# High and low part of x in one 512-column product, where one stream of tokens stands alone

## The chip, the cores and the metric

The kernel runs on one core of one Trainium2 chip. The metric is the device time of one execution in microseconds (us); the kernel before took 2060.02 us (median of 3 runs, 2059.41 to 2060.64). The engines are named as the profile names them: PE is TensorE (its weight loads are PEld), DVE is VectorE, ACT is ScalarE, POOL is GpSimd, SP issues most DMAs.

## The reference

The program is two transformer blocks of two layers each, on 256 tokens of width 1024, in float32. Both blocks are mostly gated feed-forward layers:

```
rmsnorm(h, g) = h * rsqrt(mean(h*h) + eps) * g
swiglu(x, w1, w3, w2) = (silu(x @ w1) * (x @ w3)) @ w2        # 1024 -> 2 x 2816 -> 1024
first block, per layer:  h = h + 0.5 * swiglu(rmsnorm(h, g0), ...)
                         h = h + mixer(rmsnorm(h, g1))         # attention of two kinds
                         h = h + 0.5 * swiglu(rmsnorm(h, g2), ...)
second block, per layer: x = layer_norm(ALPHA*x + gate1 * mixing(modulate(x)))
                         x = layer_norm(ALPHA*x + gate2 * swiglu_2(modulate(x), ...))
                         # the same for a context stream of 256 tokens, in the first layer alone
```

The second block's shifts, scales and gates ("modulation") come from a product of a vector with `w_mod`, 1024 x 6144 per layer.

## The kernel before

**Products.** Activations lie feature-major: 128 features on the partitions, 256 tokens (S) in the columns. A weight block is 128 x 128. Float32 is reached with three products of a faster type (FR): weight and activation are each split into a high part and the rest (low part), and `mm3` (L317 to L326) issues high x high, high x low, low x high, which add into one PSUM bank (L324, L325, L326). Each is a matmul with its own weight load. In most layers x has 256 columns; where both streams of the second block share a layer's weights, 512.

**Weights.** `Weights` streams one array in chunks of 8 blocks (128 x 1024, 512 KB), in the order in which they are used. Three staging tiles `wst` are filled by DMA; `prepare` makes the high part `whi` on ACT (L279) and the low part `wlo` on DVE (L280). Four chunks of split weights are kept (NHL = 4): the fifth chunk is split when PE has done with one of the four. There are 540 chunks.

**Feed-forward layers.** Up: for each of 22 hidden blocks j, `slab_fm` runs 8 k-blocks for both halves (c = 0, 1) into one bank, with the weights stored so that k=0 of c=0, k=0 of c=1, k=1 of c=0 and so on follow each other. In the first block (`ffn1_layer`, four layers, h0, h2, h3 and h5) DVE then multiplies the bank with the norm's factor `r` (L863), ACT takes the silu (L865), DVE the product (L866), and `split` makes high and low of the result (L330 on ACT, L331 on DVE). In the second block (`up_gen`) ACT and DVE read the bank directly (L1508, L1509). Down: for each of 8 output blocks m, 22 (or 11) k-blocks go into the first half of a bank, and DVE adds it to the residual (L797, L1543); in layers that follow at once, ACT and DVE then make high and low of the next input (`HI`, `LO`: L513, L514).

**Beside the layers.** `self.bg` holds background work that `step()` pushes on after each j and m: in the first three layers the product with `w_mod` (DVE L724, ACT L727, POOL L728), in the fourth (h5) the norm of the context stream (`ctx_init`: a sum on DVE, L1443 and L1445, one matmul with ones, L1447, then eight blocks of L1452 and further work).

**Order.** The build hands all instructions to a scheduler that simulates the engines with costs of its own and writes each engine's queue in the order in which its simulation starts them. On the chip each queue runs strictly in that order. PSUM has 4 banks under the name mm, 3 under sc (also used as st and tp) and one, half.

## Time and profile before

| | |
|---|---|
| runs shown | 2059.41, 2060.02, 2060.64 us |
| profiled execution | 2062.72 us, of which the span of instructions is 2060.9 us |
| PE busy | 1989.5 us (97%), 15355 matmuls in the profile |
| weight loads busy | 1851.9 us (90%) |
| DVE busy | 1524.9 us (74%) |
| ACT busy | 1134.6 us (55%) |
| DMA | 172 GB/s on average |
| granted clock of TensorE, mean | 0.988 |

An engine's busy time is the union of its instructions. Matmuls overlap in the profile (each row shows its whole passage), so PE can look busy without running at its best: what a product costs is read from the distance of the starts of two that follow each other. A row of the timeline gives start and duration in us, then engine, line, operation, out<-in by the program's names and the shape, partitions x elements.

### The profile page before, as it was taken

To read this page: it belongs to the slowest core of one execution; us is meant where nothing else is said; L and a number is where in the kernel's file an instruction comes from. 1 tells how busy PE (TensorE), PEld (TensorE's weight loads), DVE (VectorE), ACT (ScalarE), POOL (GpSimd) and SP (SyncE) were. 2 spreads that over 40 slices of the span, in tenths; PEclk is the share of its full clock that TensorE was granted. 3 is DMA by queue.
4 is the path that set the end of the run, shared out by engine and by line. 5 is a ranking of instruction groups with operands and counts; after the bars stand their busy time and mean duration, and the time that the engine had idled before them with its cause. 6 is when DMAs were issued, how large, how long until landed. Compare 5 with 4: busy or idle time off the path is not lost. (4 is left out here: it accounts for less than half of the span.)

```text
span 2060.9 us, 39210 instructions
## 1 busy us (share of the span) xinstructions
PE 1989.5 (97%) x15355; PEld 1851.9 (90%) x15355; DVE 1524.9 (74%) x2680; ACT 1134.6 (55%) x2028; POOL 408.4 (20%) x305
## 2 busy tenths in 40 slices
PE   8998999999999999999999999999999999989997
PEld 8988999989999998999999777988888889869997
DVE  6797797998599768886686978666665679776554
ACT  5464587555466548555556866533443455855443
POOL 1223041321033111210330112302230013112002
PEclk9999999999999999999999999999999999999999
DMA  6785645876577563556642323475555653125553
GB/s 219 260 266 171 202 144 184 281 249 215 185 232 229 187 216 110 184 172 188 188 145 73 104 80 118 144 250 169 160 163 164 216 169 103 50 83 156 183 183 103
DMA packets 117114, 355.39 MB, mean 172 GB/s; under 512 B 21782, under 2 KB 27625, under 8 KB 116481
## 3 DMA queue, kind: packets, MB, share of 16 engines
q1 hardware_dynamic: 115472, 344.54, 51.9%
q10 hardware_dynamic: 1456, 8.36, 1.1%
q8 instruction: 120, 1.97, 0.4%
q14 instruction: 66, 0.53, 0.1%
HBM read 351.66 MB, written 8.90 MB: 175 GB/s over the span
## 5 line engine op out<-in xcount | busy, mean ns | idle before, releaser
L280 DVE TENSOR_TENSOR wlo<-wst,whi 128x1024 fp32r<-128x1024 f32 x540 | 709.2, 1314 | 329.4 <-ACT whi L279 327.1
L324 PE MATMUL mm<-HI,whi 128*128 128x256 f32 (+1 forms) x2944 | 865.2, 296 | 12.7 <-ACT whi L279 8.4
L326 PE MATMUL mm<-HI,wlo 128*128 128x256 f32 (+1 forms) x2944 | 863.9, 294 | 6.0 <-DVE wlo L280 6.0
L325 PE MATMUL mm<-LO,whi 128*128 128x256 f32 (+1 forms) x2944 | 865.4, 295 | 1.0 <-DVE LO L1413 0.9
L279 ACT ACTIVATE whi<-wst 128x1024 fp32r<-128x1024 f32 x540 | 570.2, 1056 | 524.8 <-PE mm L325 292.7
L324 PEld LDWEIGHTS mm<-HI,whi 128*128 128x128 f32 x2944 | 564.2, 193 | 38.3 <-issue 11.4
L326 PEld LDWEIGHTS mm<-HI,wlo 128*128 128x128 f32 x2944 | 566.1, 192 | 21.8 <-DVE wlo L280 7.3
L325 PEld LDWEIGHTS mm<-LO,whi 128*128 128x128 f32 x2944 | 566.6, 193 | 18.7 <-issue 6.9
L326 PE MATMUL mm<-ghi,wlo 128*128 128x256 f32 (+1 forms) x1000 | 289.1, 289 | 4.7 <-DVE wlo L280 4.7
L324 PE MATMUL mm<-ghi,whi 128*128 128x256 f32 (+1 forms) x1000 | 287.7, 289 | 1.3 <-ACT ghi L330 1.3
L325 PE MATMUL mm<-glo,whi 128*128 128x256 f32 (+1 forms) x1000 | 288.6, 289 | 0.2 <-DVE glo L331 0.2
L728 POOL TENSOR_TENSOR macc<-macc,mp 128x1024 f32<-128x1024 f32 (+1 forms) x70 | 167.9, 2398 | 447.2 <-ACT mp L727 298.1
L326 PEld LDWEIGHTS mm<-ghi,wlo 128*128 128x128 f32 x1000 | 192.8, 193 | 8.4 <-DVE wlo L280 5.1
L324 PEld LDWEIGHTS mm<-ghi,whi 128*128 128x128 f32 x1000 | 192.4, 193 | 4.3 <-issue 1.5
L325 PEld LDWEIGHTS mm<-glo,whi 128*128 128x128 f32 x1000 | 192.7, 193 | 2.8 <-issue 1.1
L724 DVE SCALAR_TENSOR_TENSOR macc<-mw,sc,macc 128x512 f32<-128x512 f32 (+1 forms) x126 | 168.3, 1336 | 25.6 <-DMA mw<-in_wmod 20.4
L325 PE MATMUL mm<-wlo,HI 128*128 128x256 f32 x352 | 100.6, 286 | 4.0 <-DVE wlo L280 4.0
L324 PE MATMUL mm<-whi,HI 128*128 128x256 f32 x352 | 101.1, 288 | 0.0
L326 PE MATMUL mm<-whi,LO 128*128 128x256 f32 x352 | 100.2, 286 | 0.0
L727 ACT ACTIVATE mp<-mw,sc 128x1024 f32<-128x1024 f32 (+1 forms) x70 | 67.4, 973 | 27.5 <-DMA mw<-in_wmod 18.5
L527 POOL TENSOR_TENSOR sacc<-sacc,w 128x256 f32<-128x256 f32 x36 | 33.6, 932 | 236.7 <-ACT w L523 235.5
L330 ACT ACTIVATE ghi<-w 128x256 fp32r<-128x256 f32 (+1 forms) x120 | 51.1, 426 | 49.8 <-DVE w L866 47.1
(425 smaller groups left out, 2502.5 us busy)
## 6 DMA issues: line engine op xcount, KB each, us to landing
wst<-in_wall SPq DMA_DIRECT2D x540, 512.0 KB
mw<-in_wmod SPq DMA_DIRECT2D x48, 512.0 KB
mw<-in_wmod SPq DMA_DIRECT2D x96, 256.0 KB
brep<-bvec ACTq DMA_DIRECT2D x16, 384.0 KB
nab<-rrep SPq DMA_DIRECT2D x24, 96.0 KB
bias<-brep SPq DMA_DIRECT2D x4, 512.0 KB
bias<-brep SPq DMA_DIRECT2D x8, 256.0 KB
rrep<-in_rpb ACTq DMA_DIRECT2D x4, 348.8 KB
```

The costliest lines, as they stand in the source:

```text
L279: self.marks.append(self.nc.scalar.activation(hi, src, AF.Copy))
L280: self.nc.vector.tensor_tensor(lo, src, hi.bitcast(FT), op=OP.subtract)
L324: nc.tensor.matmul(ps, wh, xh, start=first, stop=False, skip_group_check=True)
L325: nc.tensor.matmul(ps, wh, xl, start=False, stop=False, skip_group_check=True)
L326: self.last = nc.tensor.matmul(ps, wl, xh, start=False, stop=last, skip_group_check=True)
L330: self.marks = [self.nc.scalar.activation(hi, src, AF.Copy), self.nc.vector.tensor_tensor(lo, src, hi.bitcast(FT), op=OP.subtract)]
L527: nc.gpsimd.tensor_tensor(st["acc"], st["acc"], sq, op=OP.add)
L724: nc.vector.scalar_tensor_tensor(acc[:, i], w, s, acc[:, i], op0=OP.mult, op1=OP.add)
L727: nc.scalar.activation(t, w, AF.Copy, scale=s)
L728: nc.gpsimd.tensor_tensor(acc[:, i], acc[:, i], t, op=OP.add)
```

## The change

- Where only one stream is multiplied, x is stored with high and low side by side (256 + 256 columns), and `mm3` issues two products a block in place of three: low weight x high x into the first half of a bank, then high weight x both (512 columns) into the whole bank. The bank then holds the sum in two halves, which have to be added.
- It applies in: the down projections of all four layers of the first block; the up projection of the fourth (h5), which has no product with `w_mod` beside it; the one-stream up projections of the second block (12 hidden blocks in its first layer, 22 in its second); and its one-stream down projections.
- Down: DVE adds both halves to the residual, one instruction each. Up: `joined` copies one half out on ACT and adds the other on DVE. Each half (c = 0, 1) is a bank of its own, and the weights are stored with the 8 k-blocks of c=0 first, so that a bank belongs to one chunk. In h5 and in the second block's second layer every third such bank is taken from sc.
- In h5 (`normed_up`) the first four hidden blocks multiply with `r` after the join; meanwhile, after j=1 and j=2, a normalised copy of the input is made (`xn`: one DVE instruction, one on ACT and one on DVE for each of 8 m), and from j=4 on the products read that, so the multiplication with `r` falls away.

```diff
+def _ffn1s(w1, w3, j0, j1):
+    out = []
+    for j in range(j0, j1):
+        for w in (w1, w3):
+            out.append(w[:, j * 128:(j + 1) * 128].reshape(KB, 128, 128).transpose(1, 0, 2))
+    return out
...
-        hi = self.split.tile([128, 1024], FR, name="whi")
-        lo = self.split.tile([128, 1024], FR, name="wlo")
-        self.marks.append(self.nc.scalar.activation(hi, src, AF.Copy))
-        self.nc.vector.tensor_tensor(lo, src, hi.bitcast(FT), op=OP.subtract)
-        self.hl[i] = (hi, lo)
+        w = self.split.tile([128, 2, 1024], FR, name="whl")
+        self.marks.append(self.nc.scalar.activation(w[:, 0], src, AF.Copy))
+        self.nc.vector.tensor_tensor(w[:, 1], src, w[:, 0].bitcast(FT), op=OP.subtract)
+        self.hl[i] = w
...
     def mm3(self, ps, w, x, first, last, swap=False):
-        (wh, wl), (xh, xl) = w, x
         nc = self.nc
         if swap:
-            (wh, wl), (xh, xl) = (xh, xl), (wh, wl)
+            w, x = x, w
+        wh, wl = w[:2]
+        xh, xl = x[:2]
+        if len(ps.shape) == 2 and len(xh.shape) == 2 and ps.shape[1] == 2 * xh.shape[1]:
+            nc.tensor.matmul(ps[:, :S], wl, xh, start=first, stop=False, skip_group_check=True)
+            self.last = nc.tensor.matmul(ps.rearrange("p (h t) -> p h t", h=2), wh, x[2], start=False, stop=last,
+                                         skip_group_check=True)
+            return
         nc.tensor.matmul(ps, wh, xh, start=first, stop=False, skip_group_check=True)
         nc.tensor.matmul(ps, wh, xl, start=False, stop=False, skip_group_check=True)
         self.last = nc.tensor.matmul(ps, wl, xh, start=False, stop=last, skip_group_check=True)
...
+    def wide(self, x, n, spare=False):
+        ps = self.ps("sc" if spare and self.turn % 3 == 2 else "mm")
+        self.turn += 1
+        for k in range(n):
+            self.mm3(ps, self.W.block(self.wpos + k), self.at(x, k), k == 0, k == n - 1)
+        self.wpos += n
+        return ps
+    def joined(self, dst, ps):
+        c = self.w1()
+        self.nc.scalar.activation(c, ps[:, S:], AF.Copy)
+        self.nc.vector.tensor_tensor(dst, ps[:, :S], c, op=OP.add)
...
-                nc.vector.scalar_tensor_tensor(hm, ps, scale, hm, op0=OP.mult, op1=OP.add)
+                for c in (0, S):
+                    nc.vector.scalar_tensor_tensor(hm, ps[:, c:c + S], scale, hm, op0=OP.mult, op1=OP.add)
...
+    def normed_up(self, st, pool, g, gain):
+        nc = self.nc
+        x = st["hl"]
+        y = pool.tile([128, KB, 2, S], FR, name="xn")
+        y = y[:, :, 0], y[:, :, 1], y
+        turns = {1: range(4), 2: range(4, KB)}
+        for j in range(FB):
+            t = self.w2()
+            sl = self.w1()
+            for c in range(2):
+                ps = self.wide(x if j <= NORM else y, KB, True)
+                if j == 0 and c == 0:
+                    self.rms_stat(st, D)
+                self.joined(t[:, c], ps)
+                if j <= NORM:
+                    nc.vector.tensor_tensor(t[:, c], t[:, c], st["r"], op=OP.mult)
+                if c == 0:
+                    nc.scalar.activation(sl, t[:, 0], AF.Silu)
+            nc.vector.tensor_tensor(sl, sl, t[:, 1], op=OP.mult)
+            self.split(g[:, j, 0], g[:, j, 1], sl)
+            self.step()
+            for m in turns.get(j, ()):
+                w = self.w1()
+                nc.vector.scalar_tensor_tensor(w, self.h[:, m], gain[:, m:m + 1], st["r"], op0=OP.mult, op1=OP.mult)
+                self.split(y[0][:, m], y[1][:, m], w)
...
+            if idx == 3:
+                self.normed_up(st, mp, g, self.vec[:, _VEC["norm_g"] + 40:_VEC["norm_g"] + 48])
-            for j in range(FB):
+            for j in range(FB if idx < 3 else 0):
...
-                ps = self.ps("mm")[:, :S]
-                for k in range(FB):
-                    self.mm3(ps, self.W.block(self.wpos + k), (gh[:, k], gl[:, k]), k == 0, k == FB - 1)
-                evict(m, ps)
-                self.wpos += FB
+                evict(m, self.wide(parts2(g), FB))
...
-                ps, = self.slab_fm([self.hl(1 - i)])
+                t = self.w2()
+                for c in range(2):
+                    self.joined(t[:, c], self.wide(self.hl(1 - i), KB, len(js) == FB))
                 sl = self.w1()
-                a, b = ps[:, 0], ps[:, 1]
+                a, b = t[:, 0], t[:, 1]
...
+                if len(streams) == 1:
+                    self.mm3(ps, w, parts(g(k, streams[0])), k == 0, k == nk - 1)
                     continue
...
-                evict(i, m, ps[:, c:c + S])
+                evict(i, m, ps[:, (1 - i) * S:(2 - i) * S] if len(streams) == 2 else ps)
```

How the queues are written, in h5's up projection. On PE at its start, before (mm_10213 is j=0, mm_10290 is j=1; the `whi` and `wlo` numbers name chunks):

```order
L324 MATMUL mm_10213<-HI_82,whi_10065 128x256
L325 MATMUL mm_10213<-LO_83,whi_10065 128x256
L326 MATMUL mm_10213<-HI_82,wlo_10066 128x256
...
L324 MATMUL mm_10290<-HI_82,whi_10148 128x256
L325 MATMUL mm_10290<-LO_83,whi_10148 128x256
...
L324 MATMUL mm_10213<-HI_82,whi_10095 128x256
```

and after (mm_9454 and mm_9487 are the two halves of j=0, sc_9521 and mm_9548 those of j=1):

```order
L351 MATMUL mm_9454<-HL_82,whl_9307 128x256
L352 MATMUL mm_9454<-HL_82,whl_9307 128x512
L351 MATMUL mm_9487<-HL_82,whl_9336 128x256
...
L351 MATMUL mm_9548<-HL_82,whl_9455 128x256
...
L585 MATMUL st_9476<-sacc_9350,ones_94 128x256
...
L351 MATMUL sc_9521<-HL_82,whl_9388 128x256
```

Before, two hidden blocks advance together over the first four k; after, three halves advance together over all k (the bank sc_9521 comes behind the matmul of the norm's statistics).

On PE around the matmul of the context's sum, before (mm_10443 is j=3, mm_10516 j=4):

```order
L326 MATMUL mm_10443<-HI_82,wlo_10371 128x256
L1447 MATMUL st_10362<-sacc_10358,ones_95 128x256
L324 MATMUL mm_10443<-HI_82,whi_10370 128x256
L325 MATMUL mm_10443<-LO_83,whi_10370 128x256
...
L324 MATMUL mm_10516<-HI_82,whi_10400 128x256
```

and after (mm_9713 is the second half of j=3, sc_9633 the second of j=2, sc_9749 and mm_9775 are j=4, mm_9810 and sc_9836 j=5):

```order
L352 MATMUL mm_9713<-HL_82,whl_9607 128x512
L1524 MATMUL st_9581<-sacc_9577,ones_94 128x256
L351 MATMUL sc_9633<-HL_82,whl_9522 128x256
...
L351 MATMUL sc_9749<-xn_9451,whl_9634 128x256
L351 MATMUL mm_9775<-xn_9451,whl_9687 128x256
...
L351 MATMUL mm_9810<-xn_9451,whl_9714 128x256
...
L351 MATMUL sc_9836<-xn_9451,whl_9750 128x256
```

The matmul of the context's sum (L1447, now L1524) stood inside j=3; now it stands behind both halves of j=3 and ahead of the second half of j=2, and behind it come four halves that read `xn`, woven k by k.

On DVE in the same place, before (L1443 and L1445 make the context's sum):

```order
L280 TENSOR_TENSOR wlo_10401<-wst_10295,whi_10400 128x1024
L331 TENSOR_TENSOR glo_10212<-w1_10353,ghi_10211 128x256
L1443 TENSOR_TENSOR sacc_10358<-cx_10287 128x256
L863 TENSOR_TENSOR w2_10430<-mm_10369,rstd_10277 128x512
L1445 TENSOR_TENSOR sacc_10358<-sacc_10358,cx_10287 128x256
```

and after (L297 is the split of weights, L915 with the L382 behind it makes `xn`, L372 is the join):

```order
L297 TENSOR_TENSOR whl_9714<-wst_9610,whl_9714 128x1024
L382 TENSOR_TENSOR ghl_9450<-w1_9520,ghl_9450 128x256
L1520 TENSOR_TENSOR sacc_9577<-cx_9516 128x256
L1522 TENSOR_TENSOR sacc_9577<-sacc_9577,cx_9516 128x256 x2
L1529 TENSOR_TENSOR ex_9517<-cx_9516,w1_9583 128x256
L915 SCALAR_TENSOR_TENSOR w1_9588<-h_83,vec_84,rstd_9479 128x256
...
L372 TENSOR_TENSOR w2_9604<-mm_9606,w1_9628 128x256
L907 TENSOR_TENSOR w2_9604<-w2_9604,rstd_9479 128x256
L297 TENSOR_TENSOR whl_9750<-wst_9637,whl_9750 128x1024
```

The context's sum now stands behind the weights of chunk whl_9714 (j=5), and `xn` behind the sum.

## Rows read from the trace of the kernel before

**Rows 1.** The page's head and its first part: busy time of each engine.

```profile
span 2060.9 us, 39210 instructions
PE 1989.5 (97%) x15355; PEld 1851.9 (90%) x15355; DVE 1524.9 (74%) x2680; ACT 1134.6 (55%) x2028; POOL 408.4 (20%) x305
```

**Rows 2.** Windows: stretch, length, then busy us (x instructions) by engine, clock, DMA.

```profile
core 0: us, PE busy (x) PEld busy (x) DVE busy (x) ACT busy (x) POOL busy (x), PEclk, DMA share, GB/s
491.90:555.30 63.40, 63.40 (x530) 63.40 (x529) 36.99 (x40) 29.21 (x38) 5.57 (x6) 1.00 0.65 216
830.00:960.70 130.70, 130.70 (x1079) 129.95 (x1078) 105.24 (x152) 73.98 (x123) 21.83 (x20) 1.00 0.57 182
...
1300.00:1320.00 20.00, 20.00 (x164) 19.20 (x163) 16.19 (x35) 12.32 (x26) 4.37 (x4) 1.00 0.47 151
1920.00:1983.00 63.00, 63.00 (x527) 63.00 (x527) 34.30 (x44) 29.32 (x45) 0.00 (x0) 1.00 0.57 184
```

**Rows 3.** Timeline of PE, the last down projection, 256 columns.

```profile
2043.79 0.28 PE L325 MATMUL mm<-glo,whi 128*128 128x256 f32 x1
...
2046.07 0.28 PE L326 MATMUL mm<-ghi,wlo 128*128 128x256 f32 x1
```

**Rows 4.** Timeline of PE, 512 columns: alone, and behind 256-column products.

```profile
1414.69 0.40 PE L324 MATMUL mm<-ghi,whi 128*128 128x512 f32 x1
...
1418.14 0.28 PE L324 MATMUL mm<-early_qcT,whi 128*128 128x256 f32 x1
...
1483.64 0.39 PE L326 MATMUL mm<-HI,wlo 128*128 128x512 f32 x1
...
1486.81 0.39 PE L325 MATMUL mm<-LO,whi 128*128 128x512 f32 x1
```

**Rows 5.** Lines by shape: xcount | busy us, mean ns (L280, L863, L331, L279: 831 to 961).

```profile
L280 DVE TENSOR_TENSOR wlo<-wst,whi 128x1024 fp32r<-128x1024 f32 x45 | 55.6, 1235 | 21.4 <-ACT whi L279 21.2
L863 DVE TENSOR_TENSOR w<-mm,rstd 128x512 f32<-128x512 f32 x22 | 15.1, 688 | 2.9 <-PE mm L326 2.9
L331 DVE TENSOR_TENSOR glo<-w,ghi 128x256 fp32r<-128x256 f32 x21 | 8.8, 418 | 0.0
...
L1509 DVE TENSOR_TENSOR w<-w,mm 128x256 f32<-128x256 f32 x34 | 14.0, 413 | 0.0
L797 DVE SCALAR_TENSOR_TENSOR h<-mm,h 128x256 f32<-128x256 f32 x24 | 10.1, 421 | 11.7 <-PE mm L326 11.7
L1543 DVE SCALAR_TENSOR_TENSOR ex<-mm,modv,ex 128x256 f32<-128x256 f32 x24 | 11.5, 480 | 22.6 <-PE mm L326 22.6
...
L1508 ACT ACTIVATE w<-mm 128x256 f32<-128x256 f32 x34 | 12.4, 366 | 0.0
L279 ACT ACTIVATE whi<-wst 128x1024 fp32r<-128x1024 f32 x45 | 47.6, 1057 | 42.9 <-PE mm L325 24.8 <-issue 15.0 <-PE st L534 1.6
```

**Rows 6.** Timeline of DVE and PE, start of h5's up projection.

```profile
832.76 3.12 DVE L514 SCALAR_TENSOR_TENSOR LO<-h,vec,HI 128x256 fp32r<-128x256 f32 x4
835.80 1.76 DVE L280 TENSOR_TENSOR wlo<-wst,whi 128x1024 fp32r<-128x1024 f32 x1
...
851.43 0.42 DVE L1445 TENSOR_TENSOR sacc<-sacc,cx 128x256 f32<-128x256 f32 x1
...
854.51 0.60 PE L1447 MATMUL st<-sacc,ones 128*128 128x256 f32 x2
```

**Rows 7.** Windows, h5's up projection where DVE is fullest.

```profile
907.90:931.30 23.40, 23.40 (x198) 23.40 (x197) 23.40 (x39) 16.34 (x26) 0.00 (x0) 1.00 0.61 188
```

**Rows 8.** Windows, start of the down projection of h0.

```profile
150.00:175.00 25.00, 19.00 (x152) 18.18 (x151) 24.96 (x17) 14.38 (x18) 17.56 (x6) 0.99 0.49 164
175.00:180.00 5.00, 4.92 (x23) 4.92 (x24) 4.53 (x7) 1.40 (x3) 0.00 (x0) 0.50 0.57 176
```

**Rows 9.** Timeline of DVE, the last residual.

```profile
2046.39 0.48 DVE L1543 SCALAR_TENSOR_TENSOR ex<-mm,modv,ex 128x256 f32<-128x256 f32 x1 [7.37 <-PE mm L326]
```

More of the change, by code (lines that the diff above doesn't have):

```diff
@@ L289, in block, with parts @@
             self.prepare()
-        hi, lo = self.hl[h]
         c = (i % 8) * 128
-        return hi[:, c:c + w * 128], lo[:, c:c + w * 128]
+        return parts(self.hl[h][:, :, c:c + w * 128])
+def parts(both):
+    return both[:, 0], both[:, 1], both
 class Body:
@@ L298, in __init__ @@
         self.last = None
+        self.turn = 0
         self.rests = [None, None]
```

134 lines of the change are left out of this document (70 added, 64 removed).

## The prediction

> **What bounds the kernel now.** The page's first part comes first: PE is busy 97% of the span, DVE 74%, ACT 55% [rows 1]. PE's share alone proves little, since its matmuls overlap, so the next view is the windows by stage: in the down projection of h2, in h5's up projection and in the last layer's up projection PE is busy for the whole stretch, while DVE has 20 to 46% of its time free [rows 2]. Then the timeline, for the distance of starts. In the last down projection 20 products of 256 columns start between 2043.79 and 2046.07, so 2.28/19 = 0.120 us each [rows 3], and the stretch of h2 (63.4 us, 528 products) gives the same 0.120. PE there goes from one product to the next with no hole: these stages last as long as their products. For 512 columns, where both streams share a layer, 15 starts lie between 1483.64 and 1486.81, 3.17/14 = 0.226 us each; where stretches of 256-column products alternate with them it is 15 in 3.45 us, 0.230 [rows 4]. Doubling the columns costs 0.106 to 0.110 us, so some 13 ns of the 0.120 belong to a product whatever its width. That part is what the change is about.
>
> **The change part by part.** *Products.* The blocks concerned: 8 x 22 in each of the four down projections of the first block (704), 22 x 16 in h5's up projection (352), 12 x 16 and 22 x 16 in the one-stream up projections of the second block (544), 2 x 8 x 11 and 8 x 22 in its one-stream down projections (352): 1952. A block costs 3 x 0.120 = 0.360 us now and 0.120 + 0.226 = 0.346 after, so it gains 13.6 ns and all of them 26.5 us. Bounds: with 0.230 for the wide product 10 ns or 19.5 us, with 0.118 for the narrow one (0.344) 15.6 ns or 30.5 us. I take 26.5, since 0.120 and 0.226 each come from unbroken stretches of their kind.
>
> The Trainium skill ("TensorE: Matmul & The Clock Gate", section "Back-to-back issue gap") puts the warm distance at columns / 2.4 GHz plus 2.5 ns; by it a block would go from 327.5 to 325 ns, the gain would be 4.9 us, and with the losses worked out below the sum 2067.0 us, slower than before. The rows differ from it, with 120 and 226 ns where it has 109 and 216, and they decide.
>
> *Where the gain does not count.* From 150 to 175 us the down projection of h0 is paced by DVE, busy for all of 25 us while PE gets through 152 instructions, about 50 blocks [rows 8]; their 13.6 ns are lost, 0.7 us.
>
> *Residuals.* Each m gets one more DVE instruction, 0.42 us (first block) or 0.48 (second) [rows 5]. It lies beside the next m's products (22 x 0.346 = 7.6 us) and costs nothing, except behind the very last m, where nothing is left to do but the final norm: +0.48 us [rows 9].
>
> *Joins.* Each hidden block gets two copies on ACT (0.37) and two additions on DVE (0.41); in h5 the first four get two multiplications of 0.42 in place of one of 512 columns [rows 5]. The cover is PE's 5.55 us a hidden block. In the last layer DVE is busy 34.3 of 63 us and ACT 29.3 [rows 2]; with 0.8 us more a block both stay under 75%. In the second block's first layer DVE is busy 16.2 of 20 us [rows 2] and comes to some 95%; the weights are split up to three chunks (8 us) ahead, which hides such a stretch. I take 0 (up to 3 us if that cover is gone).
>
> *The start of h5's up projection.* Here I expect a loss: the work for `xn` (16 instructions on DVE, 8 on ACT) arrives within three hidden blocks, and the written order makes PE wait for it. Before, PE waits nowhere in this stage [rows 2]. Step by step, from the order and the durations of [rows 5, 6]:
> - PE starts at 831.0 and now weaves two halves; input blocks beyond the sixth come late (DVE makes four of them until 835.9), and the third half begins with a product that reads the low weights of the fourth chunk, split on DVE until 835.80 + 1.76 = 837.5. Until then PE has 12 blocks, 4.2 us of 6.5: about 2.4 us idle. (Before, it had all of k = 0 to 3 of two hidden blocks, 16 blocks of 0.36, for that time.)
> - The three woven halves hold three of four chunks to their end, and the next chunks queue on ACT and DVE (1.06 + 1.24 us each) with joins and the norm's factor between them: 1.5 us.
> - The matmul of the context's sum now stands ahead of a whole half of j=2. PE reaches it when j=3 is done. DVE, in its queue, first has to split chunk whl_9714, whose place comes free only then: ACT 1.06, DVE 1.24, the low part of j=1's result 0.42, the sum 3 x 0.42, and hand-overs: 4.2 us idle. Before, the sum's last step started at 851.43 and PE came to the matmul at 854.51 [rows 6], no wait.
> - Behind it PE has 8 blocks that don't read `xn` and 16 that need it up to m=3 (8.3 us), then it wants m=4. From the sum to `xn` of m=4 DVE has 18 instructions of 0.42 and a split of 1.24, 8.8 us, with about 2 us of waits for ACT's parts: 2 us idle.
> - The four halves woven there end together and give their four chunks back together: the next split (1.06 + 1.24) has only three blocks (1.0 us) as cover: 1.3 us.
>
> Sum 11.4 us. Bounds: 0, if everything behind PE's waits turns out early enough, and 20, if the waits also bring the clock down: in h0 PE had a hole between 165 and 175, and the stretch after it ran at a granted clock of 0.50, 23 instructions in 5 us [rows 8].
>
> *Sum.* 26.5 - 0.7 - 0.48 - 11.4 = 13.9 us off. The profiled execution, on which all this rests, took 2062.72 us, 1.8 more than its span and 2.7 more than the median of the runs; the differences carry over: 2060.0 - 13.9 = 2046.2 us.
>
> **The rivals.**
> - *The cover holds in h5.* The scheduler wrote this order because its own simulation saw little waiting; if the real queues fit as well, only 1.2 us come off the gain: 2034.7 us. For it: DVE is on average only 105 of 131 us busy in that stage, and four hidden blocks at 100% DVE cost PE nothing before [rows 2, 7]. Against: the waits above are waits for something ordered behind something, which average load does not cure. Chance 0.24.
> - *More of it.* The same pattern (woven halves, slots that come free together) also stands at the starts of the second block's up projections; if each of the two costs another 4.5 us, 2055. Against: there DVE has no `xn` to make. Chance 0.10.
> - *Columns alone count.* If a product's cost went with its columns, a block would stay at 0.360 and only the losses would remain: 2060.0 + 0.5 + 11.4 = 2071.9 us, slower. The rows speak against it, 0.226 is not 0.240 [rows 4]. Chance 0.03.
> - *DVE becomes the bound of h5's up projection* (the slower side I hold likeliest). DVE's 105 us there [rows 2] grow by 44 joins (18.2), 8 multiplications (3.3) and 16 instructions for `xn` (6.7) and lose 22 of 0.69 (15.1 [rows 5]): 118 us, while PE's stage shrinks to 126. It decides from 126 on, 7% more than these durations; each percent beyond costs 1.2 us. To lose the other stages' gain and 4 us besides it would have to reach some 143 us, 21% more, as happens to single splits beside POOL (1.76 and not 1.24 at 835.80 [rows 6]); then 2065. POOL works 22 of the 131 us. Chance 0.05.
>
> **How the numbers follow.** My forecast gets 0.58, the rivals 0.24, 0.10, 0.03 and 0.05. 0.2% is 4.1 us, about what a measurement of this kernel can tell from no change. Faster means under 2055.9: all of the forecast, the first rival, and half of the second, 0.87; the same: the second's other half and a little of the last, 0.07; slower 0.06. The range runs from 2033, a little under the first rival, to 2056, a little over the second; the forecast's own is 2041 to 2052, with 9 to 15 us lost in h5 or the gain a few us off.
>
> **What the profile after would show.** PE's lines: 1952 products fewer, pairs whose starts are 0.120 and 0.226 apart, and the down projections of h2, h3 and h5 61.0 us long in place of 63.4. In h5's up projection: holes of PE ahead of the context's sum (4 us) and within j=4 and j=5, and a stage of about 137 us in place of 130.7 (126 if the cover holds). The forecast falls if the pair costs 0.36, if h5's stage is not longer than before, or if a stage that the change leaves alone moves by several us because the scheduler wrote its queues anew.

## The result and the profile after

| | before | after |
|---|---|---|
| runs, median (range) | 2060.3 us (2059.4 to 2062.8) | 2082.5 us (2080.7 to 2084.0) |
| profiled execution | 2062.7 us | 2082.8 us |
| granted clock, mean | 0.988 | 0.982 |

The change makes the kernel slower: the ratio of the times is 1.0109, with a 95% interval of 1.0095 to 1.0122. That is some 22 us more, where 14 us less were forecast.

The head of the page after, to be read against [rows 1]:

```profile
span 2081.0 us, 35637 instructions
PE 1988.5 (96%) x13403; PEld 1754.3 (84%) x13403; DVE 1580.8 (76%) x2850; ACT 1171.9 (56%) x2148; POOL 420.7 (20%) x305
```

Some 1950 products are gone (15355 - 13403), and PE is as long busy as before, while the span grew by 20 us. So about 20 us are new idle time of PE. That PE's busy time did not fall fits with products at half clock: mean clocks of 0.988 and 0.982 mean about 25 us more at 0.50, and a pair of products takes 0.64 us there in place of 0.35. The windows show where the time went (columns as in [rows 2]): the down projections of h2 and h3, h5's up projection, its two worst places, and the start of an up projection in the second block's first layer.

```profile
492.20:554.30 62.10, 62.10 (x354) 53.93 (x353) 40.14 (x47) 29.01 (x38) 6.10 (x6) 1.00 0.69 222
687.90:749.10 61.20, 61.20 (x355) 53.90 (x354) 41.05 (x54) 28.89 (x38) 6.13 (x6) 1.00 0.60 196
827.90:973.40 145.50, 134.03 (x716) 113.51 (x715) 111.61 (x197) 87.71 (x171) 19.85 (x20) 0.95 0.49 160
850.90:855.90 5.00, 0.11 (x2) 0.04 (x1) 3.66 (x7) 1.36 (x2) 0.00 (x0) 0.85 0.76 229
896.00:902.00 6.00, 5.91 (x19) 5.08 (x20) 2.88 (x7) 2.87 (x8) 1.61 (x3) 0.50 0.27 94
1328.70:1336.00 7.30, 3.02 (x11) 2.04 (x11) 7.15 (x18) 4.64 (x12) 2.59 (x3) 0.75 0.43 150
```

The down projections got shorter, h2's 62.1 for 63.4 us and h3's 61.2 for 63.5, which was before:

```profile
688.50:752.00 63.50, 63.50 (x532) 63.50 (x531) 38.38 (x47) 29.20 (x38) 5.57 (x6) 1.00 0.59 191
```

h5's up projection is 145.5 us long for 130.7, though DVE is busy for only 112 of them. Its waits on PE, from the view that sums waits by what ended them (engine, line, waited for: us in total, times, longest):

```profile
PE st L1524 <- DVE sacc L1522: 4.9, 1, 4.9
PE mm L351 <- DVE whl L297: 2.8, 3, 1.7
PE mm L351 <- DVE w L372: 2.8, 1, 2.8
PE sc L351 <- ACT xn L381: 0.4, 1, 0.4
```

These four are 10.9 us. The longest is the wait for the context's sum, which the prediction named; the third, 2.8 us for a join (L372), it did not name. Here it is in the timeline, on PE, then on ACT, then on DVE:

```profile
892.86 0.40 PE L352 MATMUL mm<-xn,whl 128*128 128x512 f32 x1
896.09 0.55 PE L351 MATMUL mm<-xn,whl 128*128 128x256 f32 x1 [2.83 <-DVE w L372]
896.44 0.63 PE L352 MATMUL mm<-xn,whl 128*128 128x512 f32 x1
896.87 0.42 PE L351 MATMUL mm<-xn,whl 128*128 128x256 f32 x1
897.08 0.63 PE L352 MATMUL mm<-xn,whl 128*128 128x512 f32 x1
```

```profile
893.30 1.06 ACT L296 ACTIVATE whl<-wst 128x1024 fp32r<-128x1024 f32 x1 [1.46 <-PE mm L352]
894.26 0.40 ACT L1268 ACTIVATE w<-ex 128x256 f32<-128x256 f32 x1
894.57 0.36 ACT L371 ACTIVATE w<-mm 128x256 f32<-128x256 f32 x1
```

```profile
894.39 1.23 DVE L297 TENSOR_TENSOR whl<-wst,whl 128x1024 fp32r<-128x1024 f32 x1 [0.92 <-ACT whl L296]
895.53 0.42 DVE L372 TENSOR_TENSOR w<-mm,w 128x256 f32<-128x256 f32 x1
```

The written order names what these are. On PE the halves stand as mm_9871, mm_9897, sc_9932, mm_9958, sc_10019, mm_9993 and, behind the wait, mm_10056, which needs the bank of mm_9871, since mm has four banks. On ACT (left) and DVE (right) it has:

```
L296 ACTIVATE whl_10057<-wst_9962 128x1024              L297 TENSOR_TENSOR whl_10057<-wst_9962,whl_10057 128x1024
L1268 ACTIVATE w1_9865<-ex_9517 128x256                 L372 TENSOR_TENSOR w2_9869<-mm_9871,w1_9893 128x256
L371 ACTIVATE w1_9893<-mm_9871 128x256
```

The join of mm_9871, which PE had finished five halves (14 us) earlier, stands behind the split of chunk whl_10057. That split waits until PE gives a chunk back at the end of mm_9993 (893.3). Then split on ACT, copy, split on DVE and addition run in a row, and only then PE has a bank. The loop costs PE 2.8 us here; behind it the granted clock is 0.50 for 6 us, and pairs start 0.64 us apart where they should have 0.35.

Each join cost what it was priced at [rows 5], in h5:

```profile
L372 DVE TENSOR_TENSOR w<-mm,w 128x256 f32<-128x256 f32 x29 | 12.1, 421 | 8.4 <-ACT w L371 8.3
```

Waits stand also in the second block's first layer, in a stretch (the last window above) whose mean clock is 0.75. Here is PE at the start of the second stream's hidden blocks, where the input (HL) and the weights' low parts come late:

```profile
1331.25 0.62 PE L351 MATMUL mm<-HL,whl 128*128 128x256 f32 x3 [0.96 <-ACT HL L1489]
1332.90 0.55 PE L351 MATMUL mm<-HL,whl 128*128 128x256 f32 x1 [1.03 <-DVE whl L297]
1334.93 0.80 PE L352 MATMUL mm<-HL,whl 128*128 128x512 f32 x1 [1.48 <-DVE HL L1490]
```

Next come products, PE in the down projections of h2 and of h3, and then the end of the kernel on DVE:

```profile
550.93 0.40 PE L352 MATMUL mm<-ghl,whl 128*128 128x512 f32 x1
551.16 0.28 PE L351 MATMUL mm<-ghl,whl 128*128 128x256 f32 x1
551.28 0.40 PE L352 MATMUL mm<-ghl,whl 128*128 128x512 f32 x1
...
552.70 0.40 PE L352 MATMUL mm<-ghl,whl 128*128 128x512 f32 x1
...
699.73 0.39 PE L352 MATMUL mm<-ghl,whl 128*128 128x512 f32 x1
...
703.89 0.39 PE L352 MATMUL mm<-ghl,whl 128*128 128x512 f32 x1
```

```profile
2065.82 1.00 DVE L1626 SCALAR_TENSOR_TENSOR ex<-mm,modv,ex 128x256 f32<-128x256 f32 x2 [6.78 <-PE mm L352]
```

Five pairs start between 550.93 and 552.70, so a pair costs 0.354 us in h2, not 0.346. In h3 it is twelve between 699.73 and 703.89, 0.347 us: the same alternation of shapes has two prices in one run. The last residual is two instructions in 1.00 us for one of 0.48 [rows 9].

### The profile page after: what moved, and what is told of

It reads as the page before. It is cut to its first block, busy times and chain, and to the rows that moved or that the text cites. A ratio compares the mean times of both kernels' runs of the same rounds, so it can differ in the third digit from the quotient of the medians.

```text
span 2081.0 us, 35637 instructions
## 1 busy us (share of the span) xinstructions
PE 1988.5 (96%) x13403; PEld 1754.3 (84%) x13403; DVE 1580.8 (76%) x2850; ACT 1171.9 (56%) x2148; POOL 420.7 (20%) x305
## 4 chain that ended last, share of the span: by engine, by line
PE 72%; DVE 13%; issue 5%; ACT 4%; DMA 3%; POOL 1%; SPq 0%; ACTq 0%; DVEq 0%; POOLq 0%
PE mm L352 17%; PE mm L355 12%; PE mm L357 11%; PE mm L356 11%; PE mm L351 9%; DVE whl L297 4%; DMA wst<-in_wall 3%; PE sc L352 2%; DVE macc L775 2%; ACT whl L296 2%; PE sc L351 1%; PE st L1368 1%; PE half L1721 1%; PE sc L1680 1%; PE tp L1709 1%
## 5 line engine op out<-in xcount | busy, mean ns | idle before, releaser
L297 DVE TENSOR_TENSOR whl<-wst,whl 128x1024 fp32r<-128x1024 f32 x540 | 716.6, 1328 | 264.6 <-ACT whl L296 262.9
L296 ACT ACTIVATE whl<-wst 128x1024 fp32r<-128x1024 f32 x540 | 569.8, 1056 | 429.0 <-PE mm L352 144.1
L355 PE MATMUL mm<-HL,whl 128*128 128x256 f32 (+1 forms) x2048 | 610.1, 301 | 10.8 <-ACT whl L296 8.2
L357 PE MATMUL mm<-HL,whl 128*128 128x256 f32 (+1 forms) x2048 | 610.8, 299 | 7.6 <-DVE whl L297 7.6
L356 PE MATMUL mm<-HL,whl 128*128 128x256 f32 (+1 forms) x2048 | 611.6, 299 | 0.0
L355 PEld LDWEIGHTS mm<-HL,whl 128*128 128x128 f32 x2048 | 391.8, 193 | 33.1 <-issue 9.0
L357 PEld LDWEIGHTS mm<-HL,whl 128*128 128x128 f32 x2048 | 393.9, 193 | 23.8 <-DVE whl L297 8.9
L356 PEld LDWEIGHTS mm<-HL,whl 128*128 128x128 f32 x2048 | 394.5, 193 | 15.9 <-issue 5.4
L352 PE MATMUL mm<-ghl,whl 128*128 128x512 f32 x960 | 341.1, 399 | 0.0
L351 PE MATMUL mm<-ghl,whl 128*128 128x256 f32 x960 | 270.7, 282 | 4.2 <-DVE whl L297 4.2
L352 PEld LDWEIGHTS mm<-ghl,whl 128*128 128x128 f32 x960 | 181.6, 189 | 44.0 <-issue 1.3
L351 PEld LDWEIGHTS mm<-ghl,whl 128*128 128x128 f32 x960 | 182.5, 190 | 6.5 <-DVE whl L297 5.0
L352 PE MATMUL mm<-HL,whl 128*128 128x512 f32 x472 | 174.1, 410 | 1.7 <-DVE HL L1490 1.5
L351 PE MATMUL mm<-HL,whl 128*128 128x256 f32 x472 | 136.0, 290 | 6.6 <-DVE whl L297 5.4
L352 PEld LDWEIGHTS mm<-HL,whl 128*128 128x128 f32 x472 | 91.0, 193 | 26.8 <-issue 2.8
L356 PE MATMUL mm<-whl,HL 128*128 128x256 f32 x352 | 100.9, 287 | 4.2 <-DVE whl L297 4.2
L355 PE MATMUL mm<-whl,HL 128*128 128x256 f32 x352 | 101.5, 289 | 0.0
L351 PEld LDWEIGHTS mm<-HL,whl 128*128 128x128 f32 x472 | 92.1, 196 | 10.9 <-DVE whl L297 4.5
L357 PE MATMUL mm<-whl,HL 128*128 128x256 f32 x352 | 101.0, 288 | 0.0
```

The lines of the kernel that those rows point to most:

```text
L296: self.marks.append(self.nc.scalar.activation(w[:, 0], src, AF.Copy))
L297: self.nc.vector.tensor_tensor(w[:, 1], src, w[:, 0].bitcast(FT), op=OP.subtract)
L351: nc.tensor.matmul(ps[:, :S], wl, xh, start=first, stop=False, skip_group_check=True)
L352: self.last = nc.tensor.matmul(ps.rearrange("p (h t) -> p h t", h=2), wh, x[2], start=False, stop=last, skip_group_check=True)
L355: nc.tensor.matmul(ps, wh, xh, start=first, stop=False, skip_group_check=True)
L356: nc.tensor.matmul(ps, wh, xl, start=False, stop=False, skip_group_check=True)
```

## The experiments

Each was compared with the kernel before on the same chip; the ratios are to it. Where a stage's length is given "from split to split", it is the time between the ends of the DVE splits (L297, before L280) of its first chunk and of the next stage's first chunk. So measured, h5's up projection has 133.7 us before and 150.5 after; the one-stream up projections of the second block's first layer have 38.3 + 38.1 before and 42.5 + 49.3 after. Splits run up to four chunks ahead of the products, so a stage can gain by such a boundary what its neighbour loses. For the first layer I therefore give the stretch from split 343 to split 393 (counted from 0) as well, from its output projections to behind both stages: 243.0 us before, 251.8 after.

**Which part loses.** Five kernels, each the changed kernel with parts set back. e1_down, down projections alone:

```diff
-        return (_ffn1s if l and f else _ffn1)(w1[l, f], w3[l, f], 0, FB) + _ffn2(w2[l, f], 0, FB)
+        return _ffn1(w1[l, f], w3[l, f], 0, FB) + _ffn2(w2[l, f], 0, FB)
-                    self.joined(t[:, c], self.wide(self.hl(1 - i), KB, len(js) == FB))
+                t, = self.slab_fm([self.hl(1 - i)])
```

> The two-product form in the down projections alone (1056 blocks); all up projections, h5's too, as before with three products and the factor r behind them. Theory A (the loss of the whole change sits in the up projections): the pair gains 10 ns a block by the starts in the changed kernel's trace (117 + 233 ns against 360), 10.6 us in all, less 0.7 in h0 and 0.5 behind the last m: 2060.3 - 9.4 = 2051 us. Theory B (the products were priced right in the prediction, 13.6 ns): 14.4 - 1.2 = 13.2 off, 2047 us. Theory C (the two-column residuals or the new order of the queues cost as much as the products gain): 2057 to 2064 us.

2060.3 us, ratio 1.0009 (1.0001 to 1.0018), so neither theory A nor B but the range of theory C; e8_layout below shows one reason. e2_h5 has h5's `normed_up` again (to e1_down):

```diff
-        return _ffn1(w1[l, f], w3[l, f], 0, FB) + _ffn2(w2[l, f], 0, FB)
+        return (_ffn1s if l and f else _ffn1)(w1[l, f], w3[l, f], 0, FB) + _ffn2(w2[l, f], 0, FB)
-            for j in range(FB):
+            if idx == 3:
+                self.normed_up(st, mp, g, self.vec[:, _VEC["norm_g"] + 40:_VEC["norm_g"] + 48])
+            for j in range(FB if idx < 3 else 0):
```

> As e1 (down projections) and h5's up projection with its xn; the second block's up projections as before. Theory A (h5 loses by waits written into its own queues): e1 + 17 us, as this stage lengthened in the changed kernel (16.8), so about 2068 us, h5's up projection about 147 us long. Theory C (a chance of the order that the scheduler wrote for the whole program): the stage comes out anywhere between the prediction's rival (126 us, e1 - 5) and 147.

2072.0 us, 1.0072 (1.0058 to 1.0087); 149.7 us from split to split: theory A, with 13 us more than e1_down by the ratios where it had 17. e3_l0 has the first layer's one-stream up projections instead (to the changed kernel, beside h5 set back; in e4_l1 the condition is turned round):

```diff
-                t = self.w2()
-                for c in range(2):
-                    self.joined(t[:, c], self.wide(self.hl(1 - i), KB, len(js) == FB))
+                if len(js) == FB:
+                    t, = self.slab_fm([self.hl(1 - i)])
+                else:
+                    t = self.w2()
+                    for c in range(2):
+                        self.joined(t[:, c], self.wide(self.hl(1 - i), KB, len(js) == FB))
```

> As e1 and the one-stream up projections of the second block's first layer (12 hidden blocks); h5 and the last layer as before. Theory A (the loss there belongs to the join's banks and to the layer's start beside the work for the second stream): e1 + 15 us as in the changed kernel (4.2 + 11.2), about 2066 us. Theory C (chance of the order): e1 - 2 to e1 + 5.

2070.4 us, 1.0052 (1.0037 to 1.0068); 42.5 + 48.3 us, the stretch 252.1 for 240.7 in e1_down. That is more than theory C allowed and less than theory A's 15. e4_l1 has the last layer's:

> As e1 and the last layer's up projection (22 hidden blocks), where nothing stands beside the layer; h5 and the first layer's as before. Theory A (cover holds here): 352 blocks by 10 ns, less 1.7 us at the start, so e1 - 1.8 us (the stage took 1.75 us less in the changed kernel), about 2049 us. By the prediction's price e1 - 4.8. Theory C (joins cost by themselves wherever they are): e1 or more.

2056.4 us, 0.9991 (0.9980 to 1.0002), 3.7 us less than e1_down; the stage takes 143.2 us for 145.9. Theory C falls there; theory A (1.8) and the prediction's price (4.8) can't be told apart. e8_layout has all products in the old form and only the new tiles:

```diff
-                evict(m, self.wide(parts2(g), FB))
+                ps = self.ps("mm")[:, :S]
+                for k in range(FB):
+                    self.mm3(ps, self.W.block(self.wpos + k), self.at(parts2(g), k), k == 0, k == FB - 1)
```

> The changed layout alone: high and low parts lie in one tile (whl, HL, ghl, chl), but all products are three of 256 columns as before, and all up projections as before. In e1_down, stages that the change leaves alone moved: first mixer +2.4 us, second mixer -1.0, second block's first projections +2.8, -3.6 and +1.6, the last layer's +5.1. Theory A (the one tile for two parts changes what waits for what, and so the written order): these stages move here too, by about the same, and the time is 2058.4 + 5 to 8, about 2065 us. Theory B (they move because down projections ended earlier or the planner saw other loads): the stages stay within 0.5 us of before, 2058 us.

2063.7 us, 1.0022 (1.0012 to 1.0032). So theory A holds in size, but of the stages that moved only the first mixer is plainly the same (+2.2 us; the last layer's first projections +1.1 and not +5.1). The traces bear out the order there: DVE's instructions stand in another order in the first mixer than before, and in the old one again, but for a few, in e16_best below, where the mixer is as short as before.

By differences of ratios (of 2059 us): the layout +4.5, the down projections -2.7, h5's up +13.0, the first layer's up +8.9, the last layer's -3.7, together +20 against the 22.4 measured; each carries some 3 us of uncertainty. Much of the last layer's +5 in e1_down lies at its start, behind the down projection of the layer before. Here is PE at that place (with a window of 20 us for the clock) and DVE's `cc`, before and in e1_down:

```profile
1666.35 0.21 DVE L1346 TENSOR_TENSOR cc<-dl_x,cc 128x42 f32<-128x42 f32 x1
1676.46 0.79 PE L1394 MATMUL tp<-rows,dl_w 32*128 32x256 f32 x2 [3.78 <-DVE h L1410]
1672.00:1692.00 20.00, 16.22 (x121) 12.09 (x120) 16.63 (x50) 9.81 (x22) 8.72 (x7) 0.83 0.54 149
```

```profile
1666.79 0.39 PE L352 MATMUL mm<-ghl,whl 128*128 128x512 f32 x1
1670.27 0.20 DVE L1421 TENSOR_TENSOR cc<-dl_x,cc 128x42 f32<-128x42 f32 x1
1670.62 0.64 PE L1457 MATMUL tp<-ident,cc 128*96 128x128 f32 x2 [3.44 <-DVE cc L1421]
1671.72 0.57 PE L1461 MATMUL st<-rows,rsel 32*128 32x256 f32 x1 [0.47 <-ACT rows L1459]
...
1673.98 0.59 PE L1366 MATMUL st<-cx,lnc 128*4 128x256 f32 x1 [1.26 <-DVE st L1353]
1666.50:1686.50 20.00, 14.83 (x85) 8.94 (x85) 14.80 (x44) 7.94 (x19) 8.48 (x7) 0.66 0.44 123
```

Before, `cc` was made some 5 us ahead of the down projection's end; in e1_down it comes some 3 us behind it (its last product starts at 1666.79). So work that the projection had covered now follows it. PE waits 5.2 us in three places for 3.8 in one, and the mean clock over the 20 us is 0.66 for 0.83.

**Is it the joins?** e12_nojoin takes them out of the whole change:

```diff
-                self.joined(t[:, c], ps)
+                src = ps[:, :S]
-                    self.joined(t[:, c], self.wide(self.hl(1 - i), KB, len(js) == FB))
+                a, b = [self.wide(self.hl(1 - i), KB, len(js) == FB)[:, :S] for c in range(2)]
```

> The whole change without its joins: all products are issued, but in the up projections silu and the gate read the first half of each bank alone (so high weight x low x is left out of the result), and the copies on ACT (L371) and additions on DVE (L372) fall away. The changed kernel took 2082.5 us, with 150.5 us for h5's up projection and 42.5 + 49.3 for the two in the second block's first layer. Theory J (the joins, by their load and by the banks that wait for them, are the loss in both layers): h5 133 to 136 us, the other two about 39 + 39, in all 2048 to 2055 us. Theory B (a bank that holds one half only, and the woven order, are the loss, joins cost little): h5 145 us or more, 2072 us or more.

2058.6 us, 1.0003 (0.9992 to 1.0015): 22 us less than with the joins. h5's up projection takes 138.3 us from split to split, the first layer's two 36.7 + 41.8, and the stretch 242.7. Here are the window of h5's up projection and the wait for the context's sum in it:

```profile
827.00:960.80 133.80, 128.28 (x719) 109.39 (x718) 96.87 (x155) 75.51 (x129) 19.95 (x20) 1.00 0.53 175
PE st L1525 <- DVE sacc L1523: 1.8, 1, 1.8
```

The clock is 1.00 in this window, no wait for a bank is left, and the wait for the context's sum, which had been 4.9 us, is 1.8. So the joins carry the 22 us by which the changed kernel is slower than the one before, as theory J has it: 12 in h5, 9 in the first layer's stretch. But the total lies 4 us above theory J's range, and h5 2 us above its 133 to 136: without joins the change still gains nothing. Theory B's single banks and woven order are still in this kernel, and h5 is 4.6 us longer than before in spite of its cheaper products.

**What in a join costs?** Not `xn` or the context's sum by themselves. e5_noxn multiplies with `r` to the end, e6_ctx starts the context's norm later:

```diff
-NORM = 3
+NORM = 22
-        turns = {1: range(4), 2: range(4, KB)}
+        turns = {}
```

```diff
-                self.bg.append(self.ctx_init())
+                self.bg.append(self.ctx_init(8))
-        yield
+        for _ in range(1 + wait):
+            yield
```

Both expectations speak of a wait for `xn`, e5_noxn's of 1.9 us; the view of waits above shows 0.4 us for `xn` and 1.7 for a split of weights.

> As e2_h5 (down projections and h5's up projection), but without xn: all 22 hidden blocks of h5 multiply with r behind the join, no normalised copy is made. e2_h5 took 2072.0 us with 149.7 us between the splits of the first chunks of h5's up and down projections. Theory A (waits written into the queues: xn and the context's sum): the wait for xn (1.9) and the backlog behind it with its half clock (3.0 + 2.2) go, the wait for the context's sum (5.1 + 2.3) stays: about 142 to 143 us, 2065 us. Theory D (DVE and ACT are simply too full with joins; a bank waits for its join): more work on DVE, 150 us or more, 2072 or more.

2079.2 us, 1.0097 (1.0077 to 1.0116), 151.8 us: slower, so theory D, in its second half. DVE is not full (115.7 of 149.0 us busy), but PE waits for joins three times:

```profile
PE mm L351 <- DVE w L372: 9.6, 3, 4.6
```

> As e2_h5, but the context stream's first norm begins eight hidden blocks later, behind xn. Theory A: the wait for the context's sum with its half clock (5.1 + 2.3 us) goes, the wait for xn stays: about 142 us for the stage, 2065 us. Theory E (the start of the stage is late whatever stands in it, the sum is only where PE happens to wait): PE waits elsewhere instead, 148 us or more, 2070 us or more.

2071.3 us, 1.0058 (1.0040 to 1.0076), 147.6 us: theory E. The wait for the sum is gone, and waits for joins stand in its place:

```profile
PE mm L351 <- DVE w L372: 6.0, 3, 2.8
```

e11_bufs gives the joins buffers of their own:

```diff
-        c = self.w1()
+        c = pool.tile([128, S], FT, name="wj", bufs=4) if pool else self.w1()
-            t = self.w2()
-            sl = self.w1()
+            t = pool.tile([128, 2, S], FT, name="wt", bufs=4)
+            sl = pool.tile([128, S], FT, name="ws", bufs=4)
```

> As e2_h5, but the joins of h5 have buffers of their own (four each for the copy, the joined halves and the silu) in place of the shared rings of four (w1) and two (w2). Theory W (three of four w1 a hidden block hold the joins back): h5's up projection 142 us or less, from 149.7, and 2064 us or less. Rival D (the joins come late for the engines' load, not for buffers): 148 to 151 us, 2071 us.

2071.0 us, 1.0055 (1.0040 to 1.0070), 143.1 us: 6.6 us shorter, between the two; the total moved less. PE no longer waits for a join in this stage; 3.7 us for the context's sum and 4.4 for splits are left. DVE still has 22 us free:

```profile
827.40:966.00 138.60, 128.80 (x719) 109.74 (x718) 116.65 (x197) 88.74 (x172) 19.69 (x20) 1.00 0.52 169
```

e13_spare takes every third half of the first layer from sc:

```diff
-                        self.joined(t[:, c], self.wide(self.hl(1 - i), KB, len(js) == FB))
+                        self.joined(t[:, c], self.wide(self.hl(1 - i), KB, True))
```

> As e3_l0 (2070.4 us; up projections 42.5 + 48.3 us in the second block's first layer), but there too every third half takes a bank of sc. Theory K (four banks are two hidden blocks, and PE waits for a bank that waits for its join): the two stages fall to 80 us or less together, 2060 us. Rival (the loss is the work for the second stream's norm, which is late whatever the banks): no change, 2068 to 2072 us; or slower, where sc is missed by others.

2065.3 us, 1.0025 (1.0014 to 1.0037): 43.7 + 37.8 us, so the later stage lost its whole excess (48.3 to 37.8) and the earlier one kept it. The stretch is 246.3 us, between e3_l0's 252.1 and e1_down's 240.7. Banks are half of the answer there.

e14_joinr makes a join one instruction:

```diff
-        c = self.w1()
-        self.nc.scalar.activation(c, ps[:, S:], AF.Copy)
-        self.nc.vector.tensor_tensor(dst, ps[:, :S], c, op=OP.add)
+        self.nc.vector.tensor_reduce(dst, ps.rearrange("p (h t) -> p t h", h=2), AX.X, OP.add)
```

> The whole change (2082.5 us), but each join is one DVE reduction over the two halves of the bank in place of a copy on ACT and an addition on DVE. Theory H (the hand-over through ACT and the buffer that it needs are what makes joins late): h5's up projection 140 us or less (from 150.5), the first layer's 84 us or less (from 91.8), 2065 us or less. Rival D (DVE's load decides): a reduction of 512 columns takes longer than 0.41 us, DVE gets fuller, 2082 us or more.

2076.9 us, 1.0080 (1.0067 to 1.0093): a quarter of the loss comes back, and theory H's 2065 is not reached. h5's up projection has 145.4 us, and no wait for a join is left in it. The first layer has 35.4 + 48.3, but this is the boundary's doing: its stretch is 253.1 us, no shorter than the 251.8 of the change. The gain comes although DVE works longer on a join:

```profile
L370 DVE TENSOR_REDUCE w<-mm 128x256 f32<-128x512 f32 x83 | 56.5, 686 | 24.8 <-PE mm L352 23.8
```

e15_late lets the joins stay and takes the neighbours away:

```diff
-                self.bg.append(self.ctx_init())
+                self.bg.append(self.ctx_init(15))
-NORM = 3
+NORM = 6
-        turns = {1: range(4), 2: range(4, KB)}
+        turns = {1: range(0, 2), 2: range(2, 4), 3: range(4, 6), 4: range(6, KB)}
```

This context norm ends inside the down projection, in a tile (`ex`) which the tokens' final norm uses by then, so the second block works on other values:

> As e2_h5, but the context stream's first norm begins 15 hidden blocks later, and xn is made two m at a time behind j=1 to 4 (read from j=7 on). e6_ctx (eight blocks later, xn as in the change) had 147.6 us for h5's up projection, with two holes of 3.0 us where the context's norm ran. Theory D (wherever further work on DVE meets the joins, joins come late in the written order and PE waits for a bank): the holes in the middle go, some at the end stay, 138 to 142 us, 2062 to 2066 us. Rival (holes belong to the joins alone): 147 us or more, 2071 us.

2068.9 us, 1.0050 (1.0035 to 1.0065); 131.3 us from split to split, less than either bound expected, and less than the 133.7 before:

```profile
823.80:954.00 130.20, 126.48 (x713) 108.91 (x711) 101.17 (x170) 79.78 (x149) 9.42 (x10) 1.00 0.56 184
```

All 44 joins are in it, the context's norm is not, and PE is idle for only 3.7 us. So joins don't fill an engine; they come late where other work stands between them. The context's norm made the down projection behind it 9.9 us longer than before instead (73.7 for 63.8), so the kernel as a whole gains little. e19_wfirst tests the other suspect, that a chunk's first product now needs its low part:

```diff
-            nc.tensor.matmul(ps[:, :S], wl, xh, start=first, stop=False, skip_group_check=True)
-            self.last = nc.tensor.matmul(ps.rearrange("p (h t) -> p h t", h=2), wh, x[2], start=False, stop=last,
-                                         skip_group_check=True)
+            nc.tensor.matmul(ps.rearrange("p (h t) -> p h t", h=2), wh, x[2], start=first, stop=False,
+                             skip_group_check=True)
+            self.last = nc.tensor.matmul(ps[:, :S], wl, xh, start=False, stop=last, skip_group_check=True)
```

> The whole change (2082.5 us), with the 512-column product (high weights) ahead of the 256-column one (low weights). Theory P (PE waits for the low part of a chunk just split, 1.24 us of DVE later than the high part): the short holes at the starts of the stages (0.9 at 833 us, several around 1330) go, h5's up projection 146 us, the first layer's 88 us, in all 2074 to 2078 us. Rival J (the joins set the waits): within 3 us of 2082.5.

2082.0 us, 1.0118 (1.0101 to 1.0136): no change in all, so theory P falls as the cause of the loss. h5's up projection got longer (155.7 us and not 146), the first layer's stretch shorter (247.4 us).

**What the products give.** e7_group issues a chunk's 256-column products first, then its 512-column ones:

```diff
+            for k, w in zip(part, ws):
+                nc.tensor.matmul(ps[:, :S], w[1], xs[k][0], start=k == 0, stop=False, skip_group_check=True)
+            for k, w in zip(part, ws):
+                self.last = nc.tensor.matmul(both, w[0], xs[k][2], start=False, stop=k == n - 1, skip_group_check=True)
```

> As e4_l1 (down projections and the last layer's up projection, 1408 blocks), but within a chunk of weights first all 256-column products, then all 512-column ones. e4_l1 took 2056.4 us; h2's down projection with alternating products took 62.0 us on PE, 352 ns a pair. Theory A (a switch of width costs PE time: 117 + 233 alternating against 120 + 226 in stretches): 346 ns a pair, 6 ns by 1408 blocks or 8 us less, about 2048 to 2050 us. Theory B (the pair costs its 352 in any order): 2056 us, and a product in a stretch shows that the 226 of the both-stream layers doesn't hold for these.

2052.7 us, 0.9974 (0.9962 to 0.9986). The timeline (x8: eight in a row):

```profile
520.78 1.12 PE L379 MATMUL mm<-ghl,whl 128*128 128x256 f32 x8
521.73 2.00 PE L381 MATMUL mm<-ghl,whl 128*128 128x512 f32 x8
523.57 1.12 PE L379 MATMUL mm<-ghl,whl 128*128 128x256 f32 x8
```

0.95/8 = 0.119 and 1.84/8 = 0.230 us, so 0.349 a pair: better than the 0.354 of h2 alternating, and neither 0.346 nor better than the 0.347 of h3 alternating. From the first start to the last, h2's down projection went from 61.9 us in e4_l1 to 61.3, h3's from 61.1 to 61.4. So that a switch of width costs time (theory A) is not shown. 0.230 is the value the prediction kept as a bound [rows 4].

**Versions that beat both.** e16_best keeps what gained (down, last layer, grouped) and gives weights and compressed query two tiles again:

```diff
-        w = self.split.tile([128, 2, 1024], FR, name="whl")
+        hi = self.split.tile([128, 1024], FR, name="whi")
+        lo = self.split.tile([128, 1024], FR, name="wlo")
-            chl = ap.tile([128, 2, 2, S], FR, name="chl")
+            chl = ap.tile([128, 2, S], FR, name="cqh"), ap.tile([128, 2, S], FR, name="cql")
```

> Two products only in the down projections and in the last layer's up projection, grouped by width within a chunk (as e7_group, 2052.7 us), and the high and low parts of the weights and of the compressed query in tiles of their own again, as before. Theory L (the one-tile layout cost 4.7 us by another written order, e8_layout): 2048 us. Rival (the layout's loss is not in those tiles): 2052 to 2053 us. Predicted from prices measured so far: 1408 blocks by 11.4 ns are 16 us, less what the woven and the DVE-paced stages don't give back.

2051.2 us, 0.9961 (0.9949 to 0.9973). The first mixer is back at its length (122.5 us; 124.7 with one tile); the total gained 2.7 us on e7_group and not 4.7, between the two theories. e17_h5mild adds h5 with the edits of e11_bufs, e6_ctx and e15_late's `turns` and `NORM`:

> As e16_best, and h5's up projection in two products, with buffers of its own for the joins, xn made two m at a time, and the context's norm eight hidden blocks later. Theory D (joins are late only where other work and short buffers meet them): h5's up projection 131 to 135 us, against 133.6 with three products, and e16_best within 2 us. Rival (joins beside any other work cost): 140 us or more, e16_best + 6.

2054.8 us, 0.9977 (0.9965 to 0.9989), 138.0 us, between the two theories: most of the loss is gone, and nothing is gained. e18_bestr is e16_best with e14_joinr's edit (its only joins are the last layer's):

> As e16_best, with the joins of the last layer's up projection as one DVE reduction each. Theory H: the start of that stage, where joins and splits share ACT, gets shorter, e16_best - 1 to - 2 us. Rival D: DVE 0.3 us more a join, 44 joins, hidden under PE: e16_best within 1 us.

2048.9 us, 0.9954 (0.9941 to 0.9966), the fastest median seen. The 2.3 us to e16_best are within what two such measurements can differ by (the intervals overlap), and the stage itself did not change (141.8 us, e16_best 141.5), so theory H is not shown by it. e20_bestw turns its two loops of products (e7_group's) round:

> As e18_bestr (2048.9 us), with the 512-column products of a chunk ahead of its 256-column ones. Theory P: the low parts get 1.8 us (8 x 0.23) more time in every chunk, 1 to 3 us less, 2046 to 2048 us. Rival (splits are chunks ahead there, PE waits for none): within 1 us of 2048.9.

2052.8 us, 0.9974 (0.9963 to 0.9986): not faster, if anything slower.

## Why the prediction was wrong, point by point

- *Joins: "I take 0 (up to 3 us if that cover is gone)"*: the step that failed. Without the joins the kernel takes 2058.6 us, with them 2082.5: they cost 22 us. I compared busy times with PE's 5.55 us a hidden block, and by that measure they do fit: e15_late has all of h5's joins in 130.2 us. What I left out is that a join frees a bank, needs a work buffer, and sits in a queue written beforehand. A bank holds half a hidden block now, so six banks are three blocks (four in the first layer, two blocks) where four were four; three of the four w1 buffers go to one block. A join written behind a split that waits for PE closes a loop. Buffers, banks and the hand-over through ACT (with its buffer) were each shown to carry a part (6.6 us of h5; half of the first layer; 5.6 us in all); how they share the rest is open.
- *The start of h5's up projection, 11.4 us.* Direction right, size too small: the stage lost 16.8 from split to split, and with the cheaper products counted some 19. Term by term: the first wait for a split 0.7 us (2.4 forecast); the next chunks 0.4 (1.5); the context's sum 4.9 (4.2); `xn` 0.4 (2.0); chunks given back together 1.7 (1.3). What was missing: the bank's 2.8 us, and two stretches at clock 0.50, which I kept as a bound of 20. That the waits add up to 10.9 us, close to my 11.4, is luck: three of five terms are far smaller, and one that I did not have fills the gap. And removing the sum's place or `xn` (e6_ctx, e5_noxn) gained at most 2 us, while without joins the wait for the sum fell to 1.8: the waits were where PE met late work, not its cause.
- *More of it, 4.5 us each, "there DVE has no `xn` to make", 0.10.* In the first layer it came without `xn`, some 9 us by the ratios and by the stretch; in the last layer, with spare banks and nothing beside it, it did not, -3.7.
- *Products: 13.6 ns a block.* h2's down projection went from 63.4 to 62.1 us for 176 blocks, 7.4 ns, h3's from 63.5 to 61.2, 13 ns. So my price, from unbroken stretches of either width, was met in h3 and missed by half in h2, where the pair costs 0.354; at 7.4 ns 1952 blocks give 14 us, not 26.5. Why the same products cost more in h2 stays open. The Trainium skill ("TensorE: Matmul & The Clock Gate", section "Back-to-back issue gap"), weighed there, has by an estimate from its formula 2.5 ns a block; h2 lies about midway between it and my price. By it the forecast's sum was 2067.0, slower than before, and that outcome got no chance among the rivals.
- *Where the gain does not count.* Only h0 was named. Behind the second block's first layer more is lost than its down projections gain: the work around `cc` shown above is no longer done by their end.
- *Residuals and the tail* were right: PE is busy throughout the down projections of h2 and h3, and the end is 0.5 us longer.
- *DVE as the bound of h5* did not happen: 112 of 145.5 us busy.
- *"A stage that the change leaves alone moves by several us"* was named as what would overturn the forecast and got no price: the new tiles alone cost 4.5 us (2.5 to 6.6), with another written order.
- *The last sum*: 2060.0 - 13.9 is 2046.1 and not 2046.2; nothing hangs on it.

## What to carry to other kernels

An operation that fits under the bound engine by its duration can still cost, when it is what frees a bank or a buffer: count how many banks lie between producer and reader, and look in the written order for a reader that stands behind something that waits for the producer. Take the price of a product from stretches with the same alternation of shapes, and from more than one: it was 0.354 us a pair in one down projection and 0.347 in the next. And when a layout changes, look first whether the written order of untouched stages changes with it.

## What was not expected of the hardware

After the waits of 4.9 and 2.8 us in h5 PE's granted clock was 0.50 (the lower level, 1.2 GHz), after the one of 1.7 us that ended at 876 it stayed at 1.00. Here are windows of the changed kernel, the first behind the longest wait, the second with the shortest wait in it, and then e11_bufs: its wait of 3.7 us for the context's sum, and a window of this wait and what follows it:

```profile
856.50:860.90 4.40, 4.40 (x15) 3.74 (x14) 3.18 (x8) 2.39 (x6) 0.00 (x0) 0.50 0.11 44
874.00:878.00 4.00, 2.29 (x13) 1.74 (x12) 3.24 (x3) 2.93 (x4) 0.00 (x0) 1.00 0.25 71
855.26 0.70 PE L1524 MATMUL st<-sacc,ones 128*128 128x256 f32 x2 [3.71 <-DVE sacc L1522]
851.50:861.00 9.50, 5.79 (x34) 5.08 (x34) 7.63 (x18) 4.56 (x11) 0.00 (x0) 1.00 0.49 158
```

(The window behind the 2.8 us, 896 to 902, stands above.) So a wait of 2.8 us was followed by the half clock and one of 3.7 us was not: the length of a wait alone does not tell. Pairs 0.64 apart for 0.354 over 6 us make 2.7 us, nearly as much as the wait itself.

And a pair of products has no fixed price. In h2's down projection its distances repeat 0.350, 0.350, 0.361 us, in h3's they are 0.347 nearly throughout, with the same shapes in the same order and the clock at 1.00; what decides between them is open. The difference is of the size of what the change was meant to gain.
